# Two decoder layers on one core: the end of the expert stage rewritten, and the router loads moved

## The chip, the cores and the metric

The kernel runs on one core of a Trainium2 chip. The metric is the device time of one execution in microseconds (us). Engines are named as in the profile: PE (TensorE) does matrix products, PEld is its weight load, DVE is VectorE, ACT is ScalarE, POOL is GpSimd, SP is SyncE, which issues most DMAs. Each engine works through its own list of instructions in the order in which they were written.

## What is computed

A decoder trunk of two layers over 256 tokens of 1024 values. Each layer: a token mixer, a mixture of experts and a gated embedding, each added to h. The two parts that the change touches, cut from the reference:

```python
# experts: top-1 group, then top-2 experts of 8 in it
for e in range(N_EXPERTS):                                # 32
    he = jax.nn.silu(xt @ w1[e]) * (xt @ w3[e])           # 1024 -> 256
    y = y + comb[:, e:e + 1] * (he @ w2[e])               # 256 -> 1024
# per layer, after the experts
gate = jax.nn.sigmoid(rmsnorm(h, norm_pl[i]) @ w_pg[i])   # 1024 x 1024
h = h + gate * (p[i] @ w_pe[i])
```

Layer 0 mixes with short convolutions and stick-breaking attention (even mixer), layer 1 with a chunked gMLP (odd mixer), whose first step is `gelu(xn @ w_in)`. A final norm ends the program. All is in float32.

## The kernel before

**Weights** come in units of 1 MB through one list of loads on SP into a pool of 25 buffers of 128 x 2048. A unit's load is issued when a buffer comes free (`emit_loads`). Expert units are used as they land. Units of the mixers and of w_pg are **split**: `split_pieces` makes a high part wh on ACT (line 130 with a scale, line 132 without) and a remainder wl on DVE (lines 139, 142), in one piece or four. A product is then three: xH by wh, xL by wh, xH by wl, where xH and xL are the same split of the activations. `ahead(n)` (line 151) splits units until n stand beyond the one that was taken last; without n it is two, `AHEAD`. `take` hands out the next unit.

**The expert stage** (`moe`) takes 32 experts in eight quadruples q. Each expert has room for 32 tokens; four experts lie side by side in the 128 columns or partitions. `up` multiplies the gathered tokens xg with w1 or w3 (hps), `places` makes the scatter matrix ST and the gates gts, `hidden` and `turn_hidden` give the hidden values he and their transpose gHL, `down` multiplies with w2 (yps). For q = 0 to 6 the result, times its gate, is kept as two parts o, and `scatter` adds ST by o into the accumulator acc. These scatters wait in the list `extra` and are written behind the w3 products of the next quadruple. In the list of loads, w1 of q comes first, then w2 of q - 1, then w3 of q; w2 of q = 7 is last, and four w_pg units follow.

**Behind q = 7** `down` is called with `after`: the two halves of yps are emptied by ACT, times the gate, into oF, and between them the first w_pg unit is split in four pieces. `sums(tt, n)` multiplies ST with oF into acc, for token half tt and column half n; `add_h` (DVE, line 448) adds that to h, `square` (ACT, line 347) feeds the norm, and `turn` transposes h on PE (line 376) and makes xH by a cast on ACT (line 388) and xL on DVE (line 392). The last sum, the last two additions and the 1/rms are in `rest`.

**The gated embedding** (`per_layer`) calls `proj_rows`, which multiplies with two units, i = 0 and i = 1, for both token halves. Between its products it calls `rest` (as `mid`, after the first token half of i = 0) and `hook0` (in the second token half), which turns the second column half of h; i = 1 needs that. `proj_rows` calls `ahead()` before each unit. Then come the sigmoid and the additions to h.

**Layer 1's beginning.** On POOL's list stand two loads for the odd mixer (w_raw, wsb), then the four loads of `router_operands(1)` (lines 330 to 334), then the 1/rms of the odd mixer's norm (line 370), which scales the first gelu (line 691).

Of the kernel before, what the change touches and what calls it, by code (L numbers as in the profile page):

```python
# [15 lines left out]
P = 128  # L16
T = 256
D = 1024
# [28 lines left out]
def body(tc, x, p, norm_mix, norm_ffn, norm_pl, final_norm,  # L47
# [13 lines left out]
    def f(a):  # L61
        return a.bitcast(F32)
# [352 lines left out]
    def proj_rows(xH, xL, tag="mm", hook=None, mid=None):  # L415

        pss = [psum("pr", tag)[:, 0:512] for _ in range(2)]
        for i in range(2):
            ahead()
            wh, wl = take(512, True)  # L420
            for tt in range(2):
                rows_part(pss[tt], xH, xL, wh, wl, i, tt, slice(0, 512),
                          hook if i == 0 and tt == 1 else None)
                if i == 0 and tt == 0 and mid is not None:
                    mid()
        return pss

# [248 lines left out]

    def odd_mixer(norm, xH, xL, w_sT, b_bc, make_w_sT, wr, hook):
        rb = None
# [3 lines left out]
        for b in range(4):  # L682
            pss = proj_rows(xH, xL, ("mm", "y")[b % 2], hook=hook if b == 0 else None)
            if b == 0:
                r = norm.rstd()
            if b == 1:
                rb = norm.rows()
# [55 lines left out]
        for i in range(8):  # L743
# [4 lines left out]
            if i < 7:  # L748
                out_acc(ops, ys, i == 0, False, more=i == 6)
            else:  # L750
                lps, xc = finish_mixer(1, ops, ys, nxt, wr)
            if i < 6:
# [32 lines left out]
    def moe(li, norm, lps, xc, br):  # L785
# [142 lines left out]
        def places(q):  # L928
# [14 lines left out]
            st = act("ST", [P, T], F32R)  # L943
            nc.scalar.copy(st, ps[:, 128:128 + T])  # L944
            return gt, st
# [19 lines left out]

        def down(gs, after=None):
            pss = []
            first, ts = take_raw(4, D)
            for n in range(2):
# [3 lines left out]
                for j in range(2):  # L973
                    for e in range(4):
                        s = slice(e * CAP, (e + 1) * CAP)
                        nc.tensor.matmul(ps[s, :], gs[:, j, s], ts[e][:, j, c], start=(j == 0),  # L976
                                         stop=(j == 1))
                if after is not None:
                    after(ps, n)
            drop_raw(first, 4)  # L980
# [79 lines left out]
        for q in range(NQ):  # L1060
# [9 lines left out]
            if q == PE_AT:  # L1070
# [3 lines left out]
                for n in range(2):  # L1074
                    for tt in range(2):
                        extra.append(lambda n=n, tt=tt: embed(pT, wpe, pe, n, tt))
            p3 = up(3, q, take_raw(4, DE), 4)
            he = hidden(sl, p3)
# [15 lines left out]
        pos["hold"] = HOLD[2]  # L1094

        gs = turn_hidden(he)
        oF = big("oF", [P, D])
        gt, st = pl.pop(NQ - 1)
        st = f(st)
        nxt = Norm()  # L1100
        first = []

        def after(ps, n):
            c = slice(n * 512, (n + 1) * 512)
            nc.scalar.activation(oF[:, c], ps, AF.Copy, scale=gt[:, 0:1])

            if n == 0:
                first.extend(split_pieces(pos["split"], apart=True))
                pos["split"] += 1
            for j in (2 * n, 2 * n + 1):  # L1110
                first[j][0]()
                if n == 0:
                    first[j][1]()

        def sums(tt, n):
# [3 lines left out]
            return ps  # L1119
        down(gs, after)  # L1120
        xH = big("xTH", [P, KD, T], F32R)
        xL = big("xTL", [P, KD, T], F32R)
        pss = [sums(0, 0), sums(1, 0)]
        add_h(pss[0], 0, 0)
        nxt.square(0, 0)
        add_h(pss[1], 1, 0)
        low0 = turn(0, 0, xH, xL)
        pss.append(sums(0, 1))
        low1 = turn(1, 0, xH, xL)
        nxt.square(1, 0)  # L1130
        low0()
        first[2][1]()
        first[3][1]()
        low1()

        def rest():
# [130 lines left out]
    def turn_next(tt, n):  # L1267
        if not xT:
# [10 lines left out]
                        b_s_odd.rearrange("o g t -> o (g t)").to_broadcast([P, 1024]))  # L1279
    wr, br = router_operands(1)  # L1280

    def make_w_sT():
# [12 lines left out]

    norm, lps, xc = odd_mixer(norm, xT["h"], xT["l"], w_sT, b_bc, make_w_sT, wr, hook)
    pe, norm, pxH, pxL, rest = moe(1, norm, lps, xc, br)
    per_layer(norm, pe, pxH, pxL, rest)
# [26 lines left out]
```

## Time and profile before

| | us |
|---|---|
| median of 3 runs | 744.91 |
| the runs | 743.07, 744.91, 745.07 |
| the profiled execution | 743.51 |
| its span, first to last instruction | 741.5 |
| PE busy | 665.1 (90%) |
| DVE busy | 289.3 (39%) |
| ACT busy | 233.3 (31%) |
| DMA, mean over the span | 350 GB/s |

The busy times are means over stages that have different limits. In the timeline a row is the start and the duration in us, the engine, the line, the operation and what it writes and reads; a bracket gives the idle time ahead of it and who ended it. In tables by stretch, PEclk is the granted clock of TensorE, where 1.00 is 2.4 GHz and 0.50 is 1.2 GHz, and DMA is the mean busy share of the 16 DMA engines.

### The profile page before, as it was taken

Reading aid. Unit: us, or ns where it says so; the run is one execution under the profiler, and the core shown is the slowest. Engines: PE = TensorE matmul, PEld = TensorE weight load, DVE = VectorE, ACT = ScalarE, POOL = GpSimd, SP = SyncE. Lnnn points to the kernel's source line nnn. Section 1 sums busy time; section 2 is a strip of 40 time slices with the busy share of each in tenths; the row PEclk is TensorE's granted clock in tenths of the full one; section 3 lists DMA queues with packets and bytes.
Section 4 is the critical chain, followed back from the end, with each engine's and each line's share of the span. In section 5 each row is a group of like instructions: output and inputs, shape, how many; then the busy total and the mean of one; then the engine's idle time right before and its main releaser. Section 6 shows DMA issues by size and latency. Waiting matters only on the chain.

```text
span 741.5 us, 12330 instructions
## 1 busy us (share of the span) xinstructions
PE 665.1 (90%) x5268; PEld 491.2 (66%) x5268; DVE 289.3 (39%) x482; ACT 233.3 (31%) x338; POOL 20.2 (3%) x37
## 2 busy tenths in 40 slices
PE   8999998988889778799999999999898987977795
PEld 8989988754465534358789999987574653633365
DVE  6748733221121210157667765634121220200076
ACT  6446524111112010067543443443101022010084
POOL 3100000000000000000100000000000000000000
PEclk9999999999999998899999999999999999989799
DMA  9994598999999999999971645499999999999931
GB/s 339 367 420 180 173 428 375 382 426 426 423 427 426 426 428 423 425 408 401 378 244 54 198 162 209 146 417 426 426 426 425 426 426 425 427 426 425 420 136 57
DMA packets 61163, 259.18 MB, mean 350 GB/s; under 512 B 4308, under 2 KB 22896, under 8 KB 36272
## 3 DMA queue, kind: packets, MB, share of 16 engines
q1 hardware_dynamic: 59888, 255.35, 85.4%
q0 software_dynamic: 1072, 2.47, 0.9%
q8 instruction: 43, 0.70, 0.3%
q10 hardware_dynamic: 144, 0.52, 0.2%
q14 instruction: 16, 0.13, 0.0%
HBM read 257.28 MB, written 1.05 MB: 348 GB/s over the span
## 4 chain that ended last, share of the span: by engine, by line
PE 58%; DMA 30%; DVE 5%; issue 3%; ACT 3%; POOL 1%; POOLq 0%; SPq 0%; ACTq 0%; DVEq 0%
DMA raw<-in_moe_w_dram 27%; PE pc L411 14%; PE ops L260 9%; PE hps L923 8%; PE gat L865 8%; PE pr L260 6%; PE yps L976 3%; DMA raw<-in_w_pe_dram 3%; DVE wl L139 1%; PE gps L722 1%; PE tp L376 1%; PE lps L467 1%; PE acc L994 1%; PE acc L1117 1%; PE acc L996 1%
## 5 line engine op out<-in xcount | busy, mean ns | idle before, releaser
L923 PE MATMUL hps<-raw,xg 128*32 128x256 f32 x2048 | 141.1, 410 | 36.2 <-DMA raw<-in_moe_w_dram 21.4
L923 PEld LDWEIGHTS hps<-raw,xg 128*32 128x32 f32 x2048 | 69.3, 118 | 107.5 <-DMA raw<-in_moe_w_dram 30.9
L142 DVE TENSOR_TENSOR wl<-raw,wh 128x2048 fp32r<-128x2048 f32 (+1 forms) x45 | 95.7, 2147 | 16.6 <-ACT wh L132 15.2
L976 PE MATMUL yps<-raw,gHL 128*32 128x512 f32 x512 | 69.3, 621 | 23.7 <-ACT gHL L963 17.7
L132 ACT CAST wh<-raw 128x2048 fp32r<-128x2048 f32 (+1 forms) x41 | 74.1, 1826 | 12.2 <-DMA raw<-in_w_in_even_dram 5.7
L944 ACT CAST ST<-sl 128x256 fp32r<-128x256 f32 x16 | 6.0, 372 | 223.6 <-DVE gjunk L940 221.7
L865 PE MATMUL gat<-S,h 128*128 128x256 f32 (+1 forms) x256 | 62.8, 404 | 0.0
L865 PEld LDWEIGHTS gat<-S,h 128*128 128x128 f32 x256 | 62.0, 336 | 1.1 <-issue 0.8
L976 PEld LDWEIGHTS yps<-raw,gHL 128*32 128x32 f32 x512 | 17.0, 113 | 64.3 <-issue 29.7
L987 DVE SCALAR_TENSOR_TENSOR o<-yps,gts,o 128x512 fp32r<-128x512 f32 x28 | 20.2, 748 | 88.7 <-ACT o L986 87.7
L868 DVE TENSOR_TENSOR xg<-gat,gffn 128x512 f32<-128x512 f32 x32 | 22.1, 692 | 61.2 <-PE gat L865 57.6
L260 PE MATMUL pr<-wh,xTH 128*128 128x512 f32 (+1 forms) x152 | 40.8, 390 | 1.6 <-ACT xTH L388 1.3
L411 PE MATMUL pc<-xTH,wh 128*128 128x256 f32 x288 | 42.1, 290 | 0.1
L411 PE MATMUL pc<-xTH,wl 128*128 128x256 f32 x288 | 40.5, 284 | 0.0
L411 PE MATMUL pc<-xTL,wh 128*128 128x256 f32 x288 | 40.3, 283 | 0.0
L260 PE MATMUL pr<-wl,xTH 128*128 128x512 f32 (+1 forms) x152 | 39.6, 383 | 0.4 <-DVE wl L142 0.4
L954 DVE TENSOR_TENSOR he<-sl,hps 128x256 f32<-128x256 f32 x16 | 6.7, 422 | 83.0 <-PE hps L923 83.0
L260 PE MATMUL pr<-wh,xTL 128*128 128x512 f32 (+1 forms) x152 | 39.1, 379 | 0.0
L411 PEld LDWEIGHTS pc<-xTH,wh 128*128 128x128 f32 x288 | 38.5, 196 | 0.9 <-ACT xTH L521 0.3
L986 ACT ACTIVATE o<-yps,gts 128x512 fp32r<-128x512 f32 x28 | 18.2, 684 | 63.6 <-PE yps L976 63.6
L411 PEld LDWEIGHTS pc<-xTH,wl 128*128 128x128 f32 x288 | 37.1, 192 | 0.3
L411 PEld LDWEIGHTS pc<-xTL,wh 128*128 128x128 f32 x288 | 37.1, 192 | 0.0
(228 smaller groups left out, 813.6 us busy)
## 6 DMA issues: line engine op xcount, KB each, us to landing
raw<-in_moe_w_dram SPq DMA_DIRECT2D x192, 1024.0 KB, 19.5
raw<-in_w_in_odd_dram SPq DMA_DIRECT2D x16, 1024.0 KB, 13.2
raw<-in_w_in_even_dram SPq DMA_DIRECT2D x11, 1024.0 KB, 11.7
raw<-in_w_pg_dram SPq DMA_DIRECT2D x8, 1024.0 KB, 12.4
raw<-in_w_out_odd_dram SPq DMA_DIRECT2D x8, 1024.0 KB, 6.1
raw<-in_w_out_even_dram SPq DMA_DIRECT2D x4, 1024.0 KB, 10.8
raw<-in_w_pe_dram SPq DMA_DIRECT2D x2, 1024.0 KB, 20.3
raw<-in_w_in_even_dram SPq DMA_DIRECT2D x2, 512.0 KB, 5.8
```

Of the source, the lines that this page charges most:

```text
L132: nc.scalar.copy(wh[:, c], raw[:, c])
L139: nc.vector.scalar_tensor_tensor(wl[:, c], raw[:, c], cols[:, col + j:col + j + 1], f(wh[:, c]), op0=ALU.mult, op1=ALU.subtract)
L142: nc.vector.tensor_tensor(wl[:, c], raw[:, c], f(wh[:, c]), op=ALU.subtract)
L260: nc.tensor.matmul(ps, x, w, start=start and i == 0, stop=stop and i == 3 * n - 1)
L376: nc.tensor.transpose(tp[:, j * P:(j + 1) * P], h[:, tt, k * P:(k + 1) * P], ident)
L411: nc.tensor.matmul(o, w, xx, start=st, stop=True if first else i % (3 * KD) == 3 * KD - 1, skip_group_check=first)
L865: nc.tensor.matmul(ps[:, k], src[:, tt, k0 + k, :], S[g][:, tt, c0:c1], start=(tt == 0 and k * m % 512 == 0), stop=True, skip_group_check= ...
L868: nc.vector.tensor_tensor(xg[g][:, k0:k0 + n, c0:c1], ps, gffn[:, li, k0:k0 + n].unsqueeze(2).to_broadcast([P, n, m]), op=ALU.mult)
L923: nc.tensor.matmul(ps[e * CAP:(e + 1) * CAP, :], x[:, k, c:c + CAP], ts[e][:, k, :], start=(k == 0), stop=(k == KD - 1))
L976: nc.tensor.matmul(ps[s, :], gs[:, j, s], ts[e][:, j, c], start=(j == 0), stop=(j == 1))
L986: nc.scalar.activation(o[:, 0, c], ps, AF.Copy, scale=gt[:, 0:1])
L987: nc.vector.scalar_tensor_tensor(o[:, 1, c], ps, gt[:, 0:1], f(o[:, 0, c]), op0=ALU.mult, op1=ALU.subtract)
```

## The change

1. **Last quadruple.** Its gate goes into ST (an activation with a scale instead of a copy). The scatters of q = 6 are written ahead of the w3 products of q = 7. The down product of q = 7 is written out: three experts as before, into 96 partitions of yps; the fourth alone, as four strips of 256 columns into the four groups of 32 partitions of two tiles yq. ACT and DVE share the copies into oF.
2. **The tail.** The first w_pg unit is split behind the copies, in another order among the additions, casts and squares. In `proj_rows` with `mid`, the call of `ahead` in front of i = 0 asks for one unit, and a call of `ahead()` follows `mid()`.
3. **Router loads** of layer 1 are issued after the 1/rms of the odd mixer.

The diff, cut:

```diff
         for i in range(2):
-            ahead()
+            ahead(1 if mid is not None and i == 0 else None)
             wh, wl = take(512, True)
...
                 if i == 0 and tt == 0 and mid is not None:
                     mid()
+                    ahead()
...
             if b == 0:
                 r = norm.rstd()
+                late["r"] = router_operands(1)
...
-            nc.scalar.copy(st, ps[:, 128:128 + T])
+            if q < NQ - 1:
+                nc.scalar.copy(st, ps[:, 128:128 + T])
+            else:
+                nc.scalar.activation(f(st), ps[:, 128:128 + T], AF.Copy, scale=gt[:, 0:1])
...
+            while q == NQ - 1 and extra:
+                pop()
             p3 = up(3, q, take_raw(4, DE), 4)
...
-        def after(ps, n):
             c = slice(n * 512, (n + 1) * 512)
-            nc.scalar.activation(oF[:, c], ps, AF.Copy, scale=gt[:, 0:1])
-            if n == 0:
-                first.extend(split_pieces(pos["split"], apart=True))
-                pos["split"] += 1
-            for j in (2 * n, 2 * n + 1):
-                first[j][0]()
-                if n == 0:
-                    first[j][1]()
+            ps = psum("yps", "mm")
+            for j in range(2):
+                for e in range(3):
+                    s = slice(e * CAP, (e + 1) * CAP)
+                    nc.tensor.matmul(ps[s, :], gs[:, j, s], ts[e][:, j, c], start=(j == 0),
+                                     stop=(j == 1))
+            (nc.scalar.copy, nc.vector.tensor_copy)[n](oF[three, c], ps[three, :])
+        s = slice(3 * CAP, P)
+        qs = [psum("yq", "tp")[:, 0:256] for _ in range(2)]
+        for j in range(2):
+            for i in range(4):
+                nc.tensor.matmul(qs[i % 2][i * CAP:(i + 1) * CAP, :], gs[:, j, s],
+                                 ts[3][:, j, i * 256:(i + 1) * 256], start=(j == 0),
+                                 stop=(j == 1))
+        for i in range(4):
+            (nc.scalar.copy, nc.vector.tensor_copy)[i % 2](
+                oF[s, i * 256:(i + 1) * 256], qs[i % 2][i * CAP:(i + 1) * CAP, :])
...
         add_h(pss[0], 0, 0)
-        nxt.square(0, 0)
+        first[0][0]()
+        first[1][0]()
         add_h(pss[1], 1, 0)
+        first[0][1]()
+        first[1][1]()
         low0 = turn(0, 0, xH, xL)
         pss.append(sums(0, 1))
+        low0()
+        first[2][0]()
+        first[3][0]()
         low1 = turn(1, 0, xH, xL)
-        nxt.square(1, 0)
-        low0()
         first[2][1]()
         first[3][1]()
         low1()
+        for tt in range(2):
+            nxt.square(tt, 0)
...
-    wr, br = router_operands(1)
```

How the instructions stand on ACT behind q = 7 of layer 0, from the emptying of the down product to the last pieces of the third w_pg unit. wh_2732 (after: wh_2754) is the first unit, wh_2780 (wh_2815) the second, wh_2839 (wh_2825) the third. Before:

```order
L1105 ACTIVATE oF_2720<-yps_2738,gts_2620 128x512
L130 ACTIVATE wh_2732<-raw_2570,cols_139 128x512 x2
L347 ACTIVATE junk_2755,ss_2721<-h_72 128x512
L388 CAST xTH_2750<-tp_2758 128x4x128
L388 CAST xTH_2750<-tp_2765 128x4x128
L347 ACTIVATE junk_2771,ss_2721<-h_72 128x512
L130 ACTIVATE wh_2780<-raw_2572,cols_139 128x512 x4
L347 ACTIVATE junk_2804,ss_2721<-h_72 128x512
L347 ACTIVATE junk_2807,ss_2721<-h_72 128x512
L388 CAST xTH_2750<-tp_2821 128x4x128
L388 CAST xTH_2750<-tp_2828 128x4x128
L130 ACTIVATE wh_2839<-raw_2607,cols_139 128x512 x4
```

After:

```order
L1126 COPY oF_2720<-yq_2738 32x256 x2
L130 ACTIVATE wh_2754<-raw_2570,cols_139 128x512 x2
L388 CAST xTH_2756<-tp_2766 128x4x128
...
L388 CAST xTH_2756<-tp_2776 128x4x128
L347 ACTIVATE junk_2785,ss_2721<-h_72 128x512
...
L347 ACTIVATE junk_2809,ss_2721<-h_72 128x512
L130 ACTIVATE wh_2815<-raw_2572,cols_139 128x512 x4
L130 ACTIVATE wh_2825<-raw_2607,cols_139 128x512 x4
L388 CAST xTH_2756<-tp_2843 128x4x128
L388 CAST xTH_2756<-tp_2850 128x4x128
```

The second unit's pieces moved behind the last squares, and the third unit's moved from behind the last two casts to ahead of them. Layer 1 has the same list.

On DVE at the same place, from the first low part to the third unit's. Before:

```order
L392 TENSOR_TENSOR xTL_2751<-tp_2765,xTH_2750 128x4x128
L139 SCALAR_TENSOR_TENSOR wl_2781<-raw_2572,cols_139,wh_2780 128x512 x4
L448 TENSOR_TENSOR h_72<-h_72,acc_1554 128x512
L448 TENSOR_TENSOR h_72<-h_72,acc_1555 128x512
L369 SCALAR_TENSOR_TENSOR msq_2810<-ss_2721 128x2
L392 TENSOR_TENSOR xTL_2751<-tp_2821,xTH_2750 128x4x128
L392 TENSOR_TENSOR xTL_2751<-tp_2828,xTH_2750 128x4x128
L139 SCALAR_TENSOR_TENSOR wl_2840<-raw_2607,cols_139,wh_2839 128x512 x4
```

After:

```order
L392 TENSOR_TENSOR xTL_2757<-tp_2776,xTH_2756 128x4x128
L449 TENSOR_TENSOR h_72<-h_72,acc_1554 128x512
L449 TENSOR_TENSOR h_72<-h_72,acc_1555 128x512
L369 SCALAR_TENSOR_TENSOR msq_2812<-ss_2721 128x2
L139 SCALAR_TENSOR_TENSOR wl_2816<-raw_2572,cols_139,wh_2815 128x512 x4
L139 SCALAR_TENSOR_TENSOR wl_2826<-raw_2607,cols_139,wh_2825 128x512 x4
L392 TENSOR_TENSOR xTL_2757<-tp_2843,xTH_2756 128x4x128
L392 TENSOR_TENSOR xTL_2757<-tp_2850,xTH_2756 128x4x128
```

The additions to h moved ahead of the second unit's pieces, and the last two low parts behind the third unit's.

On POOL at the beginning of layer 1. Before:

```order
L1278 DMA wsb_2989<-in_b_s_odd_dram 128x1024
L330 DMA wr1_2993<-in_router_c_dram 128x8x4
L331 DMA wr1_2993<-in_router_f_dram 128x8x32
L333 DMA br1_2996<-in_router_c_b_dram 128x4
L334 DMA br1_2996<-in_router_f_b_dram 128x32
L370 TENSOR_TENSOR rstd_3080<-msq_3081,mhalf_111 128x2
```

After:

```order
L1301 DMA wsb_2999<-in_b_s_odd_dram 128x1024
L370 TENSOR_TENSOR rstd_3084<-msq_3085,mhalf_111 128x2
L330 DMA wr1_3088<-in_router_c_dram 128x8x4
L331 DMA wr1_3088<-in_router_f_dram 128x8x32
L333 DMA br1_3091<-in_router_c_b_dram 128x4
L334 DMA br1_3091<-in_router_f_b_dram 128x32
```

The 1/rms moved from behind the four router loads to ahead of them.

## Rows read from the trace of the kernel before

**Rows 1.** The page's part 4: the chain that ended last, by engine.

```profile
PE 58%; DMA 30%; DVE 5%; issue 3%; ACT 3%; POOL 1%; POOLq 0%; SPq 0%; ACTq 0%; DVEq 0%
```

**Rows 2.** Table by stretch: its us, PE, PEld, DVE, ACT, POOL busy, PEclk, DMA, GB/s.

```profile
307.50:311.50 4.00, 3.99 (x40) 1.91 (x44) 0.00 (x0) 0.00 (x0) 0.00 (x0) 0.53 1.02 428
398.00:480.00 82.00, 82.00 (x558) 76.08 (x557) 55.09 (x56) 37.09 (x30) 0.69 (x1) 1.00 0.45 155
500.00:702.00 202.00, 169.97 (x1614) 104.11 (x1613) 37.66 (x106) 27.83 (x53) 1.30 (x2) 0.93 1.01 425
692.30:697.00 4.70, 4.70 (x48) 2.18 (x52) 0.00 (x0) 0.00 (x0) 0.00 (x0) 0.51 1.00 424
```

**Rows 3.** The chain in time (start, us, what): the last landings, and products of the odd mixer.

```profile
305.08 12.20 DMA raw<-in_moe_w_dram
317.33 3.62 PE yps L976 x26
...
375.70 10.90 PE pr L260 x48
...
702.18 3.62 PE yps L976 x26
```

**Rows 4.** The timeline of layer 0 behind the sums, PE, DVE and ACT.

```profile
325.89 2.55 ACT L130 ACTIVATE wh<-raw,cols 128x512 fp32r<-128x512 f32 x4
...
326.63 2.74 DVE L139 SCALAR_TENSOR_TENSOR wl<-raw,cols,wh 128x512 fp32r<-128x512 f32 x4
...
327.35 1.02 PE L1117 MATMUL acc<-oF,ST 128*128 128x512 f32 x2
...
329.29 1.28 DVE L448 TENSOR_TENSOR h<-h,acc 128x512 f32<-128x512 f32 x2
...
331.45 1.06 ACT L388 CAST xTH<-tp 128x512 fp32r<-128x512 f32 x2
...
332.05 1.29 DVE L392 TENSOR_TENSOR xTL<-tp,xTH 128x512 fp32r<-128x512 f32 x2 [0.31 <-ACT xTH L388]
...
332.07 1.19 PE L260 MATMUL pr<-wh,xTH 128*128 128x512 f32 x4
...
337.84 0.69 ACT L1165 ACTIVATE gts<-pr,rstd 128x512 f32<-128x512 f32 x1 [0.79 <-PE pr L260]
```

**Rows 5.** The timeline at the end of layer 1, the last gate activation.

```profile
733.89 0.47 ACT L1165 ACTIVATE gts<-pr,rstd 128x256 f32<-128x256 f32 x1 [0.81 <-PE pr L260]
```

**Rows 6.** The timeline from the w3 products of q = 7 to the down product, layer 0.

```profile
305.07 1.06 PE L923 MATMUL hps<-raw,xg 128*32 128x256 f32 x2 [1.88 <-DMA raw<-in_moe_w_dram]
...
307.51 5.47 PE L923 MATMUL hps<-raw,xg 128*32 128x256 f32 x58 [1.38 <-DMA raw<-in_moe_w_dram]
...
313.01 0.42 DVE L954 TENSOR_TENSOR he<-sl,hps 128x256 f32<-128x256 f32 x1 [10.18 <-PE hps L923]
...
315.78 1.06 PE L976 MATMUL yps<-raw,gHL 128*32 128x512 f32 x6 [0.52 <-ACT gHL L963]
```

**Rows 7.** The timeline of PE alone, one group of up products in layer 1.

```profile
537.50 3.66 PE L923 MATMUL hps<-raw,xg 128*32 128x256 f32 x64 [1.67 <-DVE o L987]
```

**Rows 8.** The timeline at the start of the odd mixer, POOL, DVE, ACT and PE.

```profile
357.06 0.89 POOL L330 DMA_DIRECT2D wr<-in_router_c_dram  x1 [6.72 <-issue]
...
363.71 0.15 DVE L369 SCALAR_TENSOR_TENSOR msq<-ss 128x2 f32<-128x2 f32 x1
...
365.37 0.72 POOL L370 TENSOR_TENSOR rstd<-msq,mhalf 128x2 f32<-128x2 f32 x1
...
366.12 1.27 ACT L691 ACTIVATE v<-pr,rstd 128x512 f32<-128x512 f32 x2 [3.35 <-POOL rstd L370]
...
367.85 1.07 PE L260 MATMUL pr<-wl,xTH 128*128 128x512 f32 x4
...
369.23 1.20 PE L260 MATMUL pr<-wh,xTH 128*128 128x512 f32 x4 [0.32 <-ACT wh L132]
...
374.42 1.07 PE L260 MATMUL pr<-wl,xTH 128*128 128x512 f32 x4
```

More of the change, by code (lines that the diff above doesn't have):

```diff
@@ L674, in even_mixer, with odd_mixer @@
         return nxt, lps, xc
-    def odd_mixer(norm, xH, xL, w_sT, b_bc, make_w_sT, wr, hook):
+    def odd_mixer(norm, xH, xL, w_sT, b_bc, make_w_sT, late, hook):
         rb = None
@@ L750, in odd_mixer @@
             else:
-                lps, xc = finish_mixer(1, ops, ys, nxt, wr)
+                lps, xc = finish_mixer(1, ops, ys, nxt, late["r"][0])
             if i < 6:
@@ L964, in turn_hidden, with down @@
             return gs
-        def down(gs, after=None):
+        def down(gs):
             pss = []
@@ L977, in down @@
                                          stop=(j == 1))
-                if after is not None:
-                    after(ps, n)
             drop_raw(first, 4)
@@ L1097, in moe @@
         oF = big("oF", [P, D])
-        gt, st = pl.pop(NQ - 1)
-        st = f(st)
+        st = f(pl.pop(NQ - 1)[1])
         nxt = Norm()
-        first = []
-        def after(ps, n):
+        fourth, ts = take_raw(4, D)
+        three = slice(0, 3 * CAP)
+        for n in range(2):
             c = slice(n * 512, (n + 1) * 512)
-            nc.scalar.activation(oF[:, c], ps, AF.Copy, scale=gt[:, 0:1])
-            if n == 0:
-                first.extend(split_pieces(pos["split"], apart=True))
-                pos["split"] += 1
-            for j in (2 * n, 2 * n + 1):
-                first[j][0]()
-                if n == 0:
-                    first[j][1]()
+            ps = psum("yps", "mm")
[15 more added lines that the diff above has]
+                oF[s, i * 256:(i + 1) * 256], qs[i % 2][i * CAP:(i + 1) * CAP, :])
+        drop_raw(fourth, 4)
         def sums(tt, n):
@@ L1119, in sums @@
             return ps
-        down(gs, after)
+        first = split_pieces(pos["split"], apart=True)
+        pos["split"] += 1
         xH = big("xTH", [P, KD, T], F32R)
@@ L1294, in hook @@
             turn_next(t, 1)
-    norm, lps, xc = odd_mixer(norm, xT["h"], xT["l"], w_sT, b_bc, make_w_sT, wr, hook)
-    pe, norm, pxH, pxL, rest = moe(1, norm, lps, xc, br)
+    norm, lps, xc = odd_mixer(norm, xT["h"], xT["l"], w_sT, b_bc, make_w_sT, late, hook)
+    pe, norm, pxH, pxL, rest = moe(1, norm, lps, xc, late["r"][1])
     per_layer(norm, pe, pxH, pxL, rest)
```

## The prediction, made before the changed kernel was run

> **What bounds the kernel now.** I read the chain that ended last first. Matrix products hold 58% of it and landing weights 30% [rows 1], so no one engine is the bound; stretches are. Stage by stage: from 500 to 702 the DMA engines are full, from 398 to 480 they are at 0.45 and PE works without a pause (82.00 of 82.00) [rows 2]. So the experts wait for weights, and the odd mixer waits for PE. The edit sits on the seam, the end of each layer's expert stage. There the chain goes from the landing of the last w2 unit (317.33 in layer 0, 702.18 in layer 1) through 3.62 us of down products to the sums that scatter them (320.95) [rows 3]. Behind that seam PE is what everything waits for: the first gate activation of the second token half starts when PE ends, not before (337.84, 0.79 of waiting on PE), and at the very end the last one does the same (733.89, 0.81) [rows 4, 5]. A microsecond that PE loses or wins behind a seam is therefore one for the end. In layer 0 it goes on through the odd mixer, and since the DMA engines only fill up again from what PE frees there, the DMA-bound stage of layer 1 starts and ends as much later.
>
> **The change, part by part.**
>
> *The last down product.* Now three experts run as before (24 instructions in eight rounds of 512 columns), and the fourth, whose weights land last, runs as four 256-column strips side by side. Units land 2.44 apart (12.20 for five), so the third is there at 314.9, and PE can take it, since it was already at these products at 315.78 and loses the scatters that stood ahead [rows 3, 6]. Eight rounds cost up to 3.62, say 3.5: 318.4. The strips are 16 instructions; with four at a time that is four rounds of 256 columns at 3.66/16 = 0.23 [rows 7], 0.9 in all: 319.3. No row shows one expert in four strips. The nearest are the up products, four experts in four strips. The bounds are 0.9 and, one after the other, 16 times 0.23 = 3.7; I take 0.9. Then two copies must empty the first half, one on ACT and one on DVE: a DVE row of as many columns on all partitions took 0.42 [rows 6], with the hand-over some 0.65. The sums start at 319.95 instead of 320.95: **1.0 earlier**, the same in layer 1.
> A page bears on this: the Trainium skill, TensorEngine Tiling (Array Packing), section PSUM Bottleneck, says that tiling quickens the products and not the emptying of PSUM, and asks for both ScalarE and VectorE. The kernel does use both; if all four copies had to be done first, the gain would be 0.6.
>
> *The gate* moves from the emptying of the down product into the scatter matrix ST. The ST activation replaces a copy of the same shape, during the wait for w3; it costs nothing there, and 0.4 if that cover were gone.
>
> *The scatters ahead of w3.* Eight products, under 2 us, move from behind the w3 products into the wait for their weights (PE idles 1.88 and 1.38 there) [rows 6]. They ended before the last landing anyway, so this saves nothing directly; the landing is what comes last.
>
> *The reordered tail.* Here the order of ACT decides. Before, the second w_pg unit's four pieces stood ahead of the last additions to h: ACT 325.89, DVE 326.63 to 329.37, and the additions only then, 329.29, though the sum they need had started at 327.35 [rows 4]. The change takes these pieces from ahead of the additions. But the call that now follows the sums asks for two units, so the listing of ACT shows **eight pieces, the second and the third unit, ahead of the two casts of xTH** that PE needs for the second half of its contraction. Before, the third unit stood behind the casts. Step by step for layer 0: on the way to the last sum PE now waits a little for ACT's third and fourth piece, which stand behind a cast, and for the low part: I estimate that 0.2 of the 1.0 is given back, so the last sum starts at 326.55 instead of 327.35 and ends about 327.6. The addition (1.28 for two) ends at 328.25. From the additions' end to the cast, with the second square, went 0.88 before (330.57 to 331.45): 329.1. Eight pieces at 2.55/4 = 0.64 take 5.1: 334.2. The cast takes 0.53 (1.06 for two): PE restarts at **334.8**. Before it restarted at 332.07 [rows 4]. It is through with what stands ahead by 326.55 + 4.4 = 330.95 (4.72 went by between the same two points before, and the cast that PE needed had ended only at 331.98, so I take 0.3 of it as waiting), so it idles 3.85. DVE is later still: eight pieces at 2.74/4 = 0.685 from the first ACT piece (329.75) end at 335.25, the low part of the first cast (1.29 for two) at 335.9, and PE, which wants it after four products, waits 0.25 more. So PE is **3.0 later** at the end of this half, with the earlier seam counted in. What was moved forward buys nothing: the third unit's pieces were hidden behind PE before. Layer 1 has the same list, and its end also hangs on PE [rows 5]: 3.0 again.
>
> *The clock.* After idle stretches of PE the granted clock falls from 2.4 to 1.2 GHz. After waits of 1.88 and 1.38 [rows 6] the products of 307.5 to 311.5 ran at a mean of 0.53, and those of 692.3 to 697.0 at 0.51 [rows 2]; after a single idle of 1.67 the clock stayed (64 products in 3.66, against 5.47 for 58 at 307.51) [rows 6, 7]. An idle of 3.85 is longer than all of them. At half speed for about 4 us after the restart PE loses 2.0; 0.25 of that lies in the wait for the low part, and a fall early in the gap shortens it. I take **1.55 for each layer**, bounds 0 and 2.4 (4.7 halved).
> The Trainium skill, TensorE: Matmul & The Clock Gate, section HAM oscillation — how this bites in real kernels, says the same of a kernel that waits between bursts: the idle engine is gated to half and the next burst starts slow. By that rule the sum is 751.5, without it 748.4. The rows at 307.5 and 692.3 agree with the rule.
>
> *Router loads.* On POOL the 1/rms of the odd mixer stood behind four loads, the first issued at 357.06 after 6.72 of waiting, and ran at 365.37. Its input was there at 363.86 (363.71 + 0.15), behind a DVE subtraction. ACT's first gelu waited until 366.12, and PE then waits for what ACT and DVE do next, first at 369.23. From 367.85 to 374.42 six groups of four products go by, 6.57; at the pace of the 48 behind them (10.90, so 0.91 a group) they are 5.46: 1.1 lost [rows 3, 8]. With the loads behind it, 1/rms runs at about 364.0 and ACT 1.3 earlier, more than PE lost: **1.1 saved**, bounds 0 and 1.1. What is late next is the DVE subtraction ahead of the mean square. The loads themselves slip by some 8 us on an otherwise idle queue; the router reads them more than 100 us later.
>
> **The sum.** The profiled execution took 743.51, and 743.51 + 3.0 - 1.1 + 3.0 + 2 x 1.55 = 751.5. The median of the runs, 744.91, lies 1.4 above that execution, and one run of three below it; I add half: **752.2**.
>
> **The rivals.**
> *The clock stays up.* The gap is once, not repeated, like the 1.67. Then the sum is 748.4, with half the offset 749.1. Against it: the gap is more than double.
> *The clock falls in the last down product as well.* With the scatters gone from behind w3, PE has little to do from its end to the third w2 unit, up to 2 us; if w3's products then ran at full clock and the fall comes here, the eight rounds cost up to 2.2 more: 754.4 for one layer, 756.6 for two. For it: gaps of 1.88 had a fall. Against: if w3 runs slow as before, there is no such gap.
> *Only the second unit stands ahead of the casts*, as the words of the change say. Four pieces fewer are 2.55, PE restarts at 332.2, no long gap, and both seams come out even: 743.51 - 1.1 + 0.7 = 743.1. The listing speaks against it.
> *Faster.* The two seams' gains and the router's, 1.0 + 1.0 + 1.1, give 743.51 - 3.1 + 0.7 = 741.1. The place is ACT's queue between the last square and the cast: it decides whether eight pieces and a cast fit into the 1.85 that PE still has (329.1 to 330.95). That needs pieces of (1.85 - 0.53)/8 = 0.17, and they take 0.64.
>
> **How the numbers follow.** My forecast, with the clock falling after both gaps: 0.54. Clock up in one or both: 0.22. A fall in the down product on top: 0.14. Only the second unit: 0.05. Faster: 0.05. Runs tell about 0.3% (2.2 us) apart from no change, so slower holds 0.90, same 0.05, faster 0.05. The range reaches from the clock staying up, less half a term (747.5), to the fall in both down products (757.0); the unseen strips at their dear end would add 2.8 for each layer and are left out with the two last rivals.
>
> **What would show it.** In the profile after: the first sums 2.6 behind the last landing, where it was 3.6; on ACT eight wh pieces in a row and then two casts; PE's row after them with a wait of nearly 4 on ACT's xTH, in both layers; a granted clock near 0.5 for some 3 us behind it; the odd 1/rms on POOL straight behind its mean square, and no PE waits on wh and wl behind it. I am wrong if PE shows no such wait, if the pieces run during it in under 0.2 each, or if the DMA-bound stage of layer 1 does not start later by what layer 0 lost.

## The result and the profile after

The changed kernel took a median of **753.35 us** (four executions, 750.67 to 754.63) against 744.77 of the kernel before beside it: ratio 1.0115, 95% interval 1.0084 to 1.0147. It is slower, by 8.6 us; the forecast was 752.2 in a range of 747.5 to 757.0. The profiled execution is the longest of the four (754.63, span 752.7), so the traces differ by more than the medians: 741.5 to 752.7, **11.2 us**.

The seam of layer 0 in the timeline of after (start, duration, engine, line, what; in the bracket the idle time ahead and who ended it):

```profile
307.51 3.64 PE L925 MATMUL hps<-raw,xg 128*32 128x256 f32 x58 [1.37 <-DMA raw<-in_moe_w_dram]
...
314.92 4.89 PE L1115 MATMUL yps<-raw,gHL 128*32 128x512 f32 x19 [1.18 <-DMA raw<-in_moe_w_dram]
...
321.74 1.96 PE L1132 MATMUL acc<-oF,ST 128*128 128x512 f32 x4 [0.65 <-DVE oF L1126]
...
330.92 5.00 ACT L130 ACTIVATE wh<-raw,cols 128x512 fp32r<-128x512 f32 x8
...
331.66 5.39 DVE L139 SCALAR_TENSOR_TENSOR wl<-raw,cols,wh 128x512 fp32r<-128x512 f32 x8 [0.46 <-ACT wh L130]
...
335.82 1.04 ACT L388 CAST xTH<-tp 128x512 fp32r<-128x512 f32 x2
...
336.43 2.08 PE L260 MATMUL pr<-wh,xTH 128*128 128x512 f32 x4 [3.33 <-ACT xTH L388]
...
338.31 1.91 PE L260 MATMUL pr<-wh,xTL 128*128 128x512 f32 x4
...
340.01 1.91 PE L260 MATMUL pr<-wl,xTH 128*128 128x512 f32 x4
```

This answers [rows 4, 6]. Eight wh pieces stand in a row on ACT and two casts behind them; PE waits 3.33 us for the first cast and then needs 2.08, 1.91 and 1.91 for groups of four products that took 1.19, 1.08 and 1.07 behind the cast in the kernel before. The table by stretch, of after (us, PE, PEld, DVE, ACT, POOL busy, PEclk, DMA, GB/s), shows the clock; the last two stretches are layer 1:

```profile
307.50:311.50 4.00, 3.64 (x58) 1.94 (x58) 0.32 (x1) 0.00 (x0) 0.00 (x0) 1.00 1.02 428
315.00:319.00 4.00, 4.00 (x18) 1.01 (x21) 0.00 (x0) 0.48 (x1) 0.00 (x0) 0.57 1.03 407
336.40:341.00 4.60, 4.57 (x11) 3.61 (x12) 1.84 (x3) 1.95 (x3) 0.00 (x0) 0.50 1.05 405
698.30:702.00 3.70, 3.70 (x36) 1.72 (x40) 0.00 (x0) 0.00 (x0) 0.00 (x0) 0.50 1.02 430
727.40:731.00 3.60, 3.58 (x10) 2.80 (x11) 2.83 (x5) 3.32 (x7) 0.00 (x0) 0.59 0.00 0
```

Against [rows 2]: the products of w3 ran at 1.00 in layer 0, where they had run at 0.53; the fall came a stage later, in the eight rounds of the down product (0.57), and again behind the wait (0.50). Layer 1, timeline of after:

```profile
698.28 6.51 PE L925 MATMUL hps<-raw,xg 128*32 128x256 f32 x58 [1.80 <-DMA raw<-in_moe_w_dram]
...
706.34 3.21 PE L1115 MATMUL yps<-raw,gHL 128*32 128x512 f32 x21 [0.52 <-ACT gHL L969]
...
711.50 1.96 PE L1132 MATMUL acc<-oF,ST 128*128 128x512 f32 x4 [0.67 <-DVE oF L1126]
...
726.15 1.20 PE L260 MATMUL pr<-wh,xTH 128*128 128x512 f32 x4 [3.31 <-ACT xTH L388]
727.42 1.59 PE L260 MATMUL pr<-wh,xTL 128*128 128x512 f32 x4
```

Here the w3 products were the slow ones, and the wait came again, 3.31. Behind it the first group still took 1.20, as at full clock; only the groups after it were slow. In the chain in time (start, us, what) the tail of layer 0 went through PE in the kernel before:

```profile
331.28 6.54 PE pr L260 x28
```

In after it goes through ACT's pieces and the cast:

```profile
333.46 2.45 ACT wh L130 x4
335.91 0.48 ACT xTH L388
336.43 3.48 PE pr L260 x8
```

In layer 1 the chain of before ran through ACT and DVE already, from 709.6 to the end (ACT's four wh pieces, 2.46 us from 717.36, are on it); in after it goes from the split pieces and xTL into a long stretch of PE:

```profile
720.72 0.62 ACT wh L130
...
723.36 3.30 DVE wl L139 x5
...
726.68 0.70 DVE xTL L392
...
727.42 14.76 PE pr L260 x68
```

And the start of the odd mixer, timeline of after, beside [rows 8]: the 1/rms runs 0.16 behind the end of its mean square, the loads behind it.

```profile
370.82 0.15 DVE L369 SCALAR_TENSOR_TENSOR msq<-ss 128x2 f32<-128x2 f32 x1
371.13 0.71 POOL L370 TENSOR_TENSOR rstd<-msq,mhalf 128x2 f32<-128x2 f32 x1 [13.66 <-DVE msq L369]
...
372.24 0.93 POOL L330 DMA_DIRECT2D wr<-in_router_c_dram  x1 [0.41 <-issue]
```

**Where the 11.2 went.** The program is cut at five points that both traces have: the first sum of each layer (320.88 and 705.74 before; 321.74 and 711.50 after), the end of the first projection with w_pg (337.64 and 722.50; 344.77 and 733.69), and the odd mixer's gate products (471.31; 477.32).

| stretch | before | after | difference | forecast |
|---|---|---|---|---|
| start to first sum, layer 0 | 320.88 | 321.74 | +0.9 | -1.0 |
| first sum to first projection's end, layer 0 | 16.76 | 23.03 | +6.3 | +5.5 |
| from there to the odd gate products | 133.67 | 132.55 | -1.1 | -1.1 |
| from there to first sum, layer 1 | 234.43 | 234.18 | -0.3 | -1.0 |
| first sum to first projection's end, layer 1 | 16.76 | 22.19 | +5.4 | +5.5 |
| from there to the end | 19.00 | 19.01 | 0.0 | 0 |

The forecast of the tail is its 3.0 without the seam's 1.0, hence 4.0, and 1.55 for the clock. The stages that no edit touches pass the shift on unchanged: from the odd gate products to the w3 products of layer 1 that wait for the last landing it is 220.94 before (to 692.25) and 220.96 after (to 698.28). What layer 0 loses is still there at the end.

### The profile page after: what moved, and what is told of

Its sections match the earlier page's. It is cut to its first block, busy times and chain, and to the rows that moved or that the text cites. A ratio compares the mean times of both kernels' runs of the same rounds, so it can differ in the third digit from the quotient of the medians.

```text
span 752.7 us, 12376 instructions
## 1 busy us (share of the span) xinstructions
PE 668.8 (89%) x5284; PEld 495.7 (66%) x5284; DVE 292.4 (39%) x488; ACT 234.2 (31%) x340; POOL 20.2 (3%) x37
## 4 chain that ended last, share of the span: by engine, by line
PE 33%; DMA 17%; DVE 3%; ACT 1%; issue 1%; POOLq 0%; POOL 0%; ACTq 0%; SPq 0%
DMA raw<-in_moe_w_dram 16%; PE pr L260 8%; PE pc L411 6%; PE ops L260 6%; PE hps L925 5%; PE gat L867 3%; DMA raw<-in_w_in_odd_dram 1%; PE gps L724 1%; DVE wl L139 1%; DVE wl L142 1%; PE peps L260 1%; PE lps L468 1%; PE yps L982 0%; PE acc L1132 0%; PE wps L496 0%
## 5 line engine op out<-in xcount | busy, mean ns | idle before, releaser
L925 PE MATMUL hps<-raw,xg 128*32 128x256 f32 x2048 | 139.4, 410 | 34.2 <-DMA raw<-in_moe_w_dram 19.6
L982 PE MATMUL yps<-raw,gHL 128*32 128x512 f32 x448 | 57.6, 612 | 22.1 <-ACT gHL L969 16.9
L982 PEld LDWEIGHTS yps<-raw,gHL 128*32 128x32 f32 x448 | 14.7, 112 | 54.9 <-issue 25.1
L260 PE MATMUL pr<-wh,xTH 128*128 128x512 f32 (+1 forms) x152 | 42.6, 403 | 7.9 <-ACT xTH L388 7.9
L260 PE MATMUL pr<-wl,xTH 128*128 128x512 f32 (+1 forms) x152 | 41.2, 394 | 0.2 <-DVE wl L142 0.2
L260 PEld LDWEIGHTS pr<-wh,xTH 128*128 128x128 f32 x152 | 28.5, 197 | 16.1 <-ACT xTH L388 9.2
```

The costliest lines, as they stand in the source:

```text
L260: nc.tensor.matmul(ps, x, w, start=start and i == 0, stop=stop and i == 3 * n - 1)
L925: nc.tensor.matmul(ps[e * CAP:(e + 1) * CAP, :], x[:, k, c:c + CAP], ts[e][:, k, :], start=(k == 0), stop=(k == KD - 1))
```

## The experiments

The first five kernels take the change apart; the others price the clock and look for what is late next. Ratios are to the kernel before on the same chip; a ratio of 0.001 is 0.74 us.

**Only the two `ahead` calls**, in the kernel before:

```diff
         for i in range(2):
-            ahead()
+            ahead(1 if mid is not None and i == 0 else None)
...
                     mid()
+                    ahead()
```

> The kernel before with only the two calls of ahead in the projection changed: the second and the third w_pg unit are split behind the sums, all else as before. Queue theory: the whole loss is here, since nothing of the gains is: PE waits 3 to 4.5 us on the casts in both layers and then runs at half clock for 3 to 5 us; 9 to 13 us slower than before, 754 to 758. Down theory: under 3 us slower, below 748.

Measured: 753.53 us, ratio 1.0138 (1.0118 to 1.0158). Its timeline in layer 0:

```profile
329.72 5.00 ACT L130 ACTIVATE wh<-raw,cols 128x512 fp32r<-128x512 f32 x8
...
334.62 1.04 ACT L388 CAST xTH<-tp 128x512 fp32r<-128x512 f32 x2
...
335.23 1.50 PE L260 MATMUL pr<-wh,xTH 128*128 128x512 f32 x4 [3.31 <-ACT xTH L388]
```

Two lines of code hold the whole loss, and more: 10.3 us by the ratio. Its profile has them in the two tails: from the first sum to the first projection's end it is 21.67 and 21.61 instead of 16.76, and PE restarts 14.42 and 14.45 behind the first sum instead of 11.19.

**The change without the third unit**: `ahead(1)` behind `mid()`, so that four pieces stand ahead of the casts.

```diff
                     mid()
-                    ahead()
+                    ahead(1)
```

> The changed kernel with one word different: the call behind the sums asks for one unit, so only the four pieces of the second w_pg unit stand ahead of the two casts of xTH, and the third unit's stand behind them as they did in the kernel before. Queue theory (ACT's eight pieces hold the casts back and the clock falls in the gap): the wait of PE on the casts shrinks from 3.3 us to under 0.8 in both layers, the products behind it run at full clock, and some 4.5 to 5.5 us of each layer's loss go: 742 to 745 against 744.8 of before. Down theory (the rewritten last down product and the scatters ahead of w3 cost the time, since the first sums of layer 0 came 0.8 later and not 1.0 earlier): 750 to 753, as the changed kernel.

Measured: 744.18 us, ratio 1.0011 (0.9995 to 1.0028). Timeline, layer 0:

```profile
315.05 4.89 PE L1115 MATMUL yps<-raw,gHL 128*32 128x512 f32 x19 [1.15 <-DMA raw<-in_moe_w_dram]
...
334.08 1.19 PE L260 MATMUL pr<-wh,xTH 128*128 128x512 f32 x4 [0.86 <-ACT xTH L388]
```

The wait is 0.86 instead of 3.33, the group behind it takes 1.19, and 7.7 us are gone. Both runs agree: the third unit's four pieces, in front of a cast on ACT's list, are the mechanism. But the rest of the change, with the router's gain in it, comes out at nothing. The tail is still 1.2 us longer in each layer than before (17.93 and 17.97 against 16.76), the wait of 0.86 the larger part of it, and the eight rounds took 4.89 in layer 0 here too.

**The down product and the tail alone**, without the scatters ahead of w3, the `ahead` calls and the router:

```diff
-            while q == NQ - 1 and extra:
-                pop()
...
-            ahead(1 if mid is not None and i == 0 else None)
+            ahead()
...
-                    ahead()
```

> Only the rewritten last down product (three experts, then the fourth in four strips, gate in ST, copies shared by ACT and DVE, first w_pg unit split behind them): the scatters stay behind w3, the calls of ahead and the router loads are as before. Queue theory: no gap ahead of the second half, so within 1.5 us of before, 743.3 to 745.5; the sums start 0.2 to 1.0 us sooner behind the last landing. Down theory: at least 3 us slower, 748 or more.

Measured: 747.47 us, ratio 1.0049 (1.0031 to 1.0068). Timeline, layer 0:

```profile
308.62 5.50 PE L923 MATMUL hps<-raw,xg 128*32 128x256 f32 x58 [1.39 <-DMA raw<-in_moe_w_dram]
...
316.94 3.21 PE L1111 MATMUL yps<-raw,gHL 128*32 128x512 f32 x21 [0.52 <-ACT gHL L967]
...
322.10 1.96 PE L1128 MATMUL acc<-oF,ST 128*128 128x512 f32 x4 [0.67 <-DVE oF L1122]
...
332.53 1.16 PE L376 MATMUL tp<-ident,h 128*128 128x128 f32 x8 [0.88 <-DVE h L448]
```

A miss for the queue theory: the kernel is 3.6 us slower by the ratio, not within 1.5 of before, nearer to the down theory's 3 or more, and the sums of layer 0 came no sooner behind the last w3 landing (13.5, as in the kernel before, 13.4).

**The same with the scatters ahead of w3:**

```diff
+            while q == NQ - 1 and extra:
+                pop()
             p3 = up(3, q, take_raw(4, DE), 4)
```

> As the run of the down product alone, with the scatters of the seventh quadruple ahead of the last w3 too. Clock rival (with the scatters gone from behind w3, PE idles before the third w2 unit, and the clock falls inside the down product): the granted clock is 0.5 for 2 to 4 us behind 315 in layer 0, the eight rounds take some 5 us and not 3.6, and the run is 1 to 3 us slower than the one without the move. Otherwise: within 0.7 us of it, and the rounds at full clock.

Measured: 745.40 us, ratio 1.0023 (1.0009 to 1.0037). Timeline, layer 0:

```profile
314.05 3.89 PE L1113 MATMUL yps<-raw,gHL 128*32 128x512 f32 x23 [0.52 <-ACT gHL L967]
...
319.87 1.96 PE L1130 MATMUL acc<-oF,ST 128*128 128x512 f32 x4 [0.65 <-DVE oF L1124]
...
330.31 1.16 PE L376 MATMUL tp<-ident,h 128*128 128x128 f32 x8 [0.89 <-DVE h L448]
```

This is 1.9 us less than without the move, where the clock rival had 1 to 3 more: a miss as well, though the w3 products were slow here too (5.13). With the scatters behind slow w3 products PE comes to the down product 8.3 us behind the last w3 landing, too late for the strips to gain anything. With the scatters gone it comes there 6.7 behind it, and the first sum 12.5. So the forecast's 1.0 exists, and the scatters are a condition of it. In layer 1 the two stand 14.5 and 12.8 behind that landing, and the kernel before 13.5. The new tail then takes 1.2 back in each layer of both kernels (17.96 to 18.00 against 16.76); 0.9 of it is PE's wait for the last additions to h, which stand behind the split pieces on DVE.

**The router loads alone**, in the kernel before:

```diff
                 r = norm.rstd()
+                late["r"] = router_operands(1)
...
-    wr, br = router_operands(1)
```

> The kernel before with only the router loads moved behind the odd 1/rms. My theory: the odd mixer's 1/rms on POOL runs directly behind its mean square, PE's waits on the casts of the gate weights at the odd mixer's start go, and the time is 1.1 to 1.25 us under the kernel before (ratio 0.9983 to 0.9985), since everything from there to the end hangs on PE and then on DMA engines that start as much earlier. Rival: the DMA-bound stage of layer 1 starts where it did, because the loads that fill the engines hang on buffers freed elsewhere; then the gain stops at the odd mixer's end and the time is that of the kernel before, within 0.3 us.

Measured: 742.59 us, ratio 0.9979 (0.9968 to 0.9990): faster by 0.7 to 2.4 us. Timeline, the odd mixer's start:

```profile
364.95 0.15 DVE L369 SCALAR_TENSOR_TENSOR msq<-ss 128x2 f32<-128x2 f32 x1
365.25 0.71 POOL L370 TENSOR_TENSOR rstd<-msq,mhalf 128x2 f32<-128x2 f32 x1 [13.66 <-DVE msq L369]
```

Between two product groups that both traces have, 17.73 us went by before (357.73 to 375.46) and 16.60 here: 1.13. This edit alone beats both kernels.

**The clock, first attempt**: 40 products that nothing uses, in front of i = 1, on the changed kernel.

```diff
+            if mid is not None and i == 1:
+                keep_warm(40)
             wh, wl = take(512, True)
```

> The changed kernel with 40 products of 128 x 128 ones, used by nothing, added on PE where it waits for the cast of xTH in each layer's tail; the eight split pieces and all else stay. This prices the clock apart from the wait. My theory: the products take some 2.7 us of the wait of 3.3, the granted clock is 1.00 behind it instead of 0.50, and the loss from the end of the sums to the end of the first projection falls from 6.5 and 5.6 us to about 4.3 and 3.7: 749 to 750.5 in all, against 753.35 of the changed kernel. Rival 1: the clock is no part of the loss (PE would have waited on the later casts and pieces anyway); then the time stays at 753 to 753.5. Rival 2: the dummy products do not hold the clock, or lengthen the wait; then 753.5 to 755.

Measured: 760.36 us, ratio 1.0226 (1.0205 to 1.0247). Rival 2, beyond its 755, and my mistake. Timeline, layer 0:

```profile
336.10 3.97 PE L434 MATMUL wps<-ones_b 128*128 128x128 bf16 x40 [4.58 <-DVE xTL L392]
...
339.87 1.18 PE L260 MATMUL pr<-wh,xTH 128*128 128x512 f32 x4
```

The unused products write into a PSUM buffer that the casts still read, so they wait 4.58 us and stand behind the wait instead of in it. All the same they took the slow stretch on themselves: 40 of them need 3.97, where 48 need 2.85 in the second attempt, and the first useful group behind them needs 1.18.

**The clock, second attempt**: 48 such products, into the spent sums.

```diff
+            pos["spent"] = acc[0][:, 0:P]
             acc.clear()
...
+            if mid is not None and i == 1:
+                keep_warm(48, pos["spent"])
```

> The changed kernel with 48 products of 128 x 128 ones, used by nothing, on PE in the wait for the cast of xTH, as in e6_warm_gap, but written into the spent sums, whose last reader is long done, so that they need wait for nothing. In e6_warm_gap they were written into a buffer that the casts still held, and began 4.58 us late, behind the wait instead of in it. My theory: they run from 333 to 336, the granted clock is 1.00 behind them, the six groups of projections behind the wait take 5.5 us instead of 8.3 in layer 0 and as much less in layer 1, and the time is 748 to 750.5 against 753.35. Rival 1: the clock is no part of the loss; 753 to 753.5. Rival 2: with PE at full speed the wait comes back a few products later, at the low part of the cast or at the next pieces, which DVE and ACT still have ahead of them; then 751 to 753.

Measured: 749.05 us, ratio 1.0072 (1.0051 to 1.0093). Timeline, layer 0:

```profile
330.84 2.85 PE L433 MATMUL acc<-ones_b 128*128 128x128 bf16 x48
...
334.31 1.20 PE L260 MATMUL pr<-wh,xTH 128*128 128x512 f32 x4 [0.62 <-ACT xTH L388]
```

and the table by stretch of the same kernel:

```profile
334.30:340.20 5.90, 5.82 (x24) 4.51 (x25) 3.21 (x5) 2.62 (x4) 0.00 (x0) 1.00 1.05 406
722.80:728.70 5.90, 5.82 (x24) 4.49 (x25) 5.12 (x8) 4.93 (x8) 0.00 (x0) 1.00 0.01 3
```

PE restarts as late as in the changed kernel (14.65 and 14.69 behind the first sum, there 14.69 and 14.65), but the six groups behind it take 5.95 and 5.98 instead of 8.34 and 7.54. **The clock behind the wait costs 2.4 in layer 0 and 1.6 in layer 1** of the changed kernel; in the one with only the `ahead` calls, whose six groups take 7.25 and 7.16, it is 1.3 and 1.2. The time agrees, less sharply: 4.3 us lie between the medians, but they come from different chips, and by the ratios it is 3.2, with intervals that overlap. Filling the wait with work that nothing needs makes the kernel 3 to 4 us faster.

**The squares behind the casts**, on the kernel without the third unit:

```diff
-        for tt in range(2):
-            nxt.square(tt, 0)
...
-                nxt.square(tt, 1)
-            nxt.rstd()
...
                 turn(t, 1, xH, xL)()
+            for tt in range(2):
+                for n in range(2):
+                    norm.square(tt, n)
+            norm.rstd()
```

> The changed kernel with only the second w_pg unit's four pieces ahead of the casts (the third unit behind them, as in e1_second_only), and the four squares of the last normalization with their 1/rms behind the casts, where before and in e1_second_only two squares stand ahead of them on ACT. The tail's PE wait on the cast was 0.86 us in e1_second_only in both layers. My theory: that wait goes to under 0.3, the time is 0.6 to 1.4 us under e1_second_only: 742.8 to 743.6. Rival: the wait is set by the four pieces or by the additions to h on DVE, not by the squares; then it stays at 0.7 to 0.9 and the time at 744.2; or the 1/rms, now later, is waited for by the gate activations, and the time goes above 744.2.

Measured: 746.35 us, ratio 1.0029 (1.0017 to 1.0042). A miss. Timeline, layer 0:

```profile
330.87 1.07 PE L260 MATMUL pr<-wh,xTH 128*128 128x512 f32 x4
...
350.30 1.20 PE L260 MATMUL pr<-wh,xTH 128*128 128x512 f32 x4 [0.92 <-ACT wh L132]
```

The wait of 0.86 is gone (PE restarts 11.19 behind the first sum, as in the kernel before), and yet the time is not lower: the squares only moved on ACT's list, and PE now waits for ACT's pieces of later units. In layer 1 the last gate activation now starts 1.06 behind the end of PE's products, without a wait for them, and from the first projection's end to the end it takes 20.92 instead of 19.00. ACT is what is late next. The eight rounds of layer 1 took 4.89 in this profile.

**The same with unused products around the last expert**, 24 ahead of the last w3 products and 12 ahead of the last down product:

```diff
+            if q == NQ - 1:
+                keep_warm(24)
             p3 = up(3, q, take_raw(4, DE), 4)
...
         gs = turn_hidden(he)
+        keep_warm(12)
```

> e7_squares_last with products of 128 x 128 ones, used by nothing, added on PE where it waits around the last expert: 24 ahead of the last w3 products and 12 ahead of the last down product. It asks why the first sums do not start earlier in layer 0, although the scatters left the path: in the changed kernel the eight rounds of the down product took 4.89 there, with a granted clock of 0.50 to 0.67, against 3.21 with the strips alone at full clock. My theory: with PE kept busy the granted clock is 1.00 in the eight rounds in both layers, and the first sums start 1.0 to 1.7 us earlier in layer 0 and up to 1 us earlier in layer 1 than in e7_squares_last: 1 to 2 us less in all. Rival: the copies of the strips' results set the start of the sums, or the dummy products push the w3 products back; then the time is that of e7_squares_last within 0.5 us, or up to 1.5 us above it.

Measured: 745.19 us, ratio 1.0013 (1.0001 to 1.0025), 1.2 under the kernel that it rests on, with intervals that overlap. **And on the kernel without the third unit**, with the same two lines:

> e1_second_only (the changed kernel with only the second unit's four pieces ahead of the casts) with the unused products of e8_squares_last_warm around the last expert: 24 ahead of the last w3 products, 12 ahead of the last down product. In e1_second_only the profile has a granted clock of 0.50 to 0.69 in the down product of layer 0 and of 0.50 in the w3 products of layer 1. My theory: with the clock at 1.00 in both, the first sums start 5.1 us behind the landing of the third w2 unit in both layers, where the slow clock made it 6.8, and the time is 1.0 to 2.0 us under e1_second_only's 744.18, so 742.2 to 743.2, just under the kernel before: the strips' gain, kept. Rival: behind the seam ACT, not PE, is what everything waits for, as the waits of 1.1 and 0.5 us on the next unit's pieces in e7_squares_last's and e8_squares_last_warm's profile suggest; then the earlier sums buy nothing and the time is 744 within 0.5.

Measured: 743.89 us, ratio 0.9992 (0.9982 to 1.0002), by the ratios 1.4 under 1.0011. The median lies where the rival had it (744 within 0.5), on another chip, and the two intervals overlap. The traces are clearer and speak against the rival: from the first sum of layer 0 to the end it takes 420.99 here and 421.02 without the unused products, so the earlier sum arrives at the end. Timeline of this last kernel, both layers:

```profile
314.98 2.35 PE L1123 MATMUL yps<-raw,gHL 128*32 128x512 f32 x15 [1.11 <-DMA raw<-in_moe_w_dram]
...
320.11 1.96 PE L1140 MATMUL acc<-oF,ST 128*128 128x512 f32 x4 [0.65 <-DVE oF L1134]
...
698.99 3.19 PE L1123 MATMUL yps<-raw,gHL 128*32 128x512 f32 x19 [1.00 <-DMA raw<-in_moe_w_dram]
...
704.12 1.96 PE L1140 MATMUL acc<-oF,ST 128*128 128x512 f32 x4 [0.65 <-DVE oF L1134]
```

From the third w2 unit's landing (the DMA that ends PE's wait) to the first sum it is 5.13 in both layers here, 5.14 and 5.13 in the kernel with the squares moved and the same unused products, and 6.82 in the changed kernel's layer 0 (314.92 to 321.74). In the kernel before it is 6.0: 3.55 behind the fourth landing (317.33 to 320.88), which comes 2.44 after the third. So the strips gain **0.9 at full clock and lose 0.8 at half clock**. That the unused products kept the clock up here is not shown; what stays open says why.

## Why the prediction was right, and where it was off

*The mechanism* is shown: eight pieces ahead of the casts. From the first sum to the first of the eight pieces it was to be 9.15 and is 9.18; the eight take 5.00 (forecast 5.1); PE restarts 14.69 and 14.65 behind the first sum (forecast 14.85). With those pieces alone the loss is there, without the third unit it is not (PE restarts 12.20 behind the first sum, where the rival "only the second unit" had 12.25). The wait reads 3.33 and not 3.85 in the profile because PE, too, came later to it. One reading was too simple: that PE is what everything waits for behind the seam holds for layer 0, but the chain of before in the tail of layer 1 ran through ACT and DVE, and the run with the squares moved ended late although its PE was early.

*The seam* is the step that failed. "The sums start at 319.95 instead of 320.95" has its terms right: at full clock the first sum stands 5.13 behind the third landing, the forecast had 5.05, and in six profiled kernels it stands 12.49 to 12.55 behind the last w3 landing of layer 0 (forecast 12.44). But it started at 321.74, 14.23 behind that landing, in the changed kernel, since the clock was at half in the eight rounds: 4.89 against 3.19. That is the rival "the clock falls in the last down product as well", held at 14%. It came in layer 0 and cost 1.7, where I had 2.2. Its 754.4 was a median; for a profiled execution its sum is 753.7, and 754.63 was measured. In layer 1 the w3 products were slow for 6.51 instead, and the strips won 0.3. And that the scatters ahead of w3 save nothing was right only for the old down product: without that move the strips gain nothing behind slow w3 products.

*The clock behind the wait* was forecast at 1.55 a layer, within 0 and 2.4; it is 2.4 and 1.6, and 1.2 to 2.4 over the four waits that were traced. The rival "the clock stays up", 749.1, was then built, and measured 749.05; that is close by more luck than the terms have, since the clock still fell in its last down product of layer 1 (4.89), and its ratio of 1.0072 to the kernel before would be 750.1 beside 744.77.
The Trainium skill, TensorE: Matmul & The Clock Gate, section HAM oscillation — how this bites in real kernels, says that PE gated to half while it waits starts the next burst slow. Behind three of the four waits of 3.3 the traces agree: the first group took 1.50 to 2.08 (layer 0 of the changed kernel, both layers of the one with only the `ahead` calls). In layer 1 of the changed kernel the first group took 1.20 at a granted clock of 1.00, and the fall came a group later. With the unused products in the wait the granted clock was 1.00 in both layers.

*The emptying of the strips*, by which the gain was to sink if it were all waited for: it is not. The first sum starts 0.64 behind the last strip's product (319.23 to 319.87 with the scatters ahead), when one copy on each of ACT and DVE has been made; the forecast had 0.65.
The Trainium skill, TensorEngine Tiling (Array Packing), section PSUM Bottleneck, warns that behind quicker products the copy out of PSUM may become the bottleneck. The traces here show a little of it: PE waits 0.65 for the first pair of copies, where in the kernel before it went from the last product (ended 320.95) to the sums (320.88) without a wait; the second pair runs beside the first sums.

*The router loads*: 1.1 forecast, 1.12 in the changed kernel and 1.13 alone by the traces, 0.7 to 2.4 by the times. The DMA-bound stage of layer 1 passed the shift on (from the odd gate products to its last w3 products 220.94 before, 220.96 after, 221.08 with the router loads alone).

*The median* sits below the profiled execution of after and above that of before. So the loss is 11.2 by the traces, with 8.0 forecast, but 8.6 by the medians, with 7.3 forecast. The medians lie nearer to the forecast than the traces do, since the execution that was profiled is the longest of its four.

**What stays open.** Why the granted clock falls in the w3 products in one execution, in the down product in another, and in neither in a third. Up to the first sum of layer 0, five of the kernels list the same instructions: the changed one, the one without the third unit, the one with the squares moved, and the two with unused products in the tail. The eight rounds were slow in the first two, the w3 products in the third (5.33), neither in the last two. One order does show: wherever the eight rounds took 4.89, the down product of the quadruple before had been slow too, and the w3 products between them fast. The changed kernel, layer 0:

```profile
297.73 5.32 PE L982 MATMUL yps<-raw,gHL 128*32 128x512 f32 x26 [1.17 <-SPq L1006]
```

With these five and the strips with the scatters ahead there are twelve cases, two layers each. In five the down product of q = 6 took 5.32, and in four of these the eight rounds took 4.89; in the other seven it took 3.62, and the eight rounds never did. In the two kernels with unused products around the last expert it took 3.62 in both layers, so their full clock is no proof of a cure. I only argue, and no run shows, that the place of the fall explains most of the 4 us between the executions of the changed kernel.

## What to carry to other kernels

Before moving work forward, list what then stands ahead of the instruction that the bottleneck waits for, on the engine that will do it: a call that split one unit more than the next product needs cost 7.7 us here. Price a new idle stretch of PE at its length and the slow restart behind it; here a restart 3.2 to 3.5 later became 4.9 to 6.3 six groups on. When a gain must show in products that come right after a wait for weights, read the granted clock there in several executions before believing the count of products.

## What the runs showed that was not expected

- Two waits alike can have different ends: 1.18 and then 0.57 of the clock in the changed kernel, 1.18 and then 1.00 (eight rounds in 3.19) in the first kernel with unused products in the tail.
- With 48 products of 128 x 128 that nothing reads, 2.85 us of PE, in the wait, the granted clock was 1.00 behind it, and they were worth 3 to 4 us.
- A copy of 32 x 256 out of PSUM is no cheaper for its few partitions: two took 0.75 on ACT and 0.88 on DVE, so 0.37 and 0.44 each, where 256 columns on all 128 partitions took 0.37 on ACT (the copy into gHL at 315.35 in the kernel before) and 0.42 on DVE (another operation, [rows 6]).
- In the twelve profiled executions, which list the same loads up to there, the products that wait for the last w3 unit of layer 0 started between 307.16 and 308.77 (307.56 and 308.77 in the two with unused products around the last expert); a shift of 1 us in one trace is no sign of an edit.
